# Zero-padded attention scores, a mask added on VectorE, a late softmax factor, and pooled products issued between the attention steps

## The chip, the cores and the metric

The kernel runs on one core of a Trainium2 chip, as one launch. The metric is the time of that launch on the device in microseconds, the median of several runs. TensorE is called PE, VectorE DVE, ScalarE ACT, GpSimd POOL and the DMA-issuing SyncE SP, as the profile has them.

## What is computed

Two small transformer stacks one after the other on 512 tokens of width 1024, all in float32. The first has a gated mixer with a linear recurrence and a feed-forward block. The second has two layers, each a SwiGLU block, a mixer and another SwiGLU block, where a vector `c` gives shifts, scales and gates through nine modulation products per layer (`w_ada`, 2 x 36 loads of 1 MB). The mixer of its first layer is the one that matters here: differential attention beside a multi-scale pooling branch.

```python
def probs(q, k):                       # 4 heads, two score maps each, 64 wide
    sc = einsum('bhqd,bhkd->bhqk', q, k) * scale
    sc = where(mask, sc, -inf)         # causal
    return softmax(sc)
w = probs(qa, k1) - lam * probs(qb, k2)
o = rmsnorm(einsum('bhqk,bhkd->bhqd', w, v), subln_g) * (1 - lam_init)
# pooling: four groups g, windows 2, 4, 8, 16 over the tokens
d = (cumsum - lagged cumsum) / count - u[g]
p = concat(d @ pool_w[g]) * pool_scale
x = x + gate * (concat([o, p]) @ w_out)
```

## The kernel before, in words

`Net` holds the residual transposed, as 8 blocks of 128 channels by 512 tokens. A weight block comes by one DMA on SP into a staging tile (`wload`, line 99), is split there into a rounded part `whi` (ACT, line 113) and a rest `wlo` (DVE, line 114), and a product is three matmuls per 128-row slice, `whi` with both parts of the input and `wlo` with the first (`mm3`, lines 124 to 126; in token order lines 146 to 148). Each call of `wblock` also runs one waiting step of the modulation products (`ada_step`, line 181): a 1 MB load into the one tile `ada` (line 638) and two DVE passes over 1024 columns (line 640). The order on each engine is set by the tile framework's scheduler, from the order in which the program is written; each engine then runs its own list in order, and waits on the others by semaphores.

`attn` (line 665) makes q, k and v, normalises q and k, and transposes them 128 tokens at a time (`finish`, line 719) into `qT` and `kT`. In these, the 128 partitions of one head hold the first score map's 64 channels and then the second's. `pool_unit` (line 740) makes one group's input `u` (24 matmuls of 512 columns) and its window sums on POOL (line 752), and `pool_out` (line 763) multiplies by `pool_w` (line 767).

The attention itself is 16 steps, (query block i, head h), i from 3 down to 0. Step s issues four stages, each of another step: `stA` of step s, `stB` of s-1, `stC` of s-2, `stD` of s-3. One score tile of `stA`, with n = 128 (i + 1) keys, is

```python
nc.tensor.matmul(ps[:, 0:i * 128], lhsT=ql, rhs=kr[pr, h % 2, 0:i * 128], ...)       # 64 rows, L790
nc.tensor.matmul(ps[:, i * 128:n], lhsT=ql, rhs=kr[pr, h % 2, i * 128:n], ...)       # 64 rows, L791
nc.tensor.matmul(ps[:, i * 128:n], lhsT=self.ident, rhs=cm, start=False, stop=True)  # mask, L792
```

followed by the row maximum (DVE, line 793) and the exponential with its sum (ACT, line 795). There are two tiles per step, 32 in all, in 5 PSUM buffers (`acc`). `stB` normalises and subtracts the two maps (DVE, lines 803 to 806) and transposes the result (PE, line 810; ACT, line 812). `stC` multiplies by v (PE, line 819) and normalises (ACT 822, DVE 85, POOL 86, DVE 824). `stD` transposes into `oT` (PE 830, ACT 833, DVE 834). After the steps 2, 6, 10 and 14 the loop issues one `pool_out`, and after the first three of these a whole `pool_unit`; the first `pool_unit` stands ahead of the loop. The output product (`down`, line 248) follows.

Of the kernel before, what the change touches and what calls it, by code (L numbers as in the profile page):

```python
# [9 lines left out]
F32 = mybir.dt.float32  # L10
F32R = mybir.dt.float32r
U8 = mybir.dt.uint8
AF = mybir.ActivationFunctionType
# [13 lines left out]
class Net:  # L27
    def __init__(self, ctx, tc, a, out):
        self.ctx, self.tc, self.nc, self.a, self.out = ctx, tc, tc.nc, a, out
        pool = lambda name, bufs, **kw: ctx.enter_context(tc.tile_pool(name=name, bufs=bufs, **kw))  # L30
        self.const = pool("const", 1)
        self.act = pool("act", 20)
        self.xv = pool("xv", 4)
        self.stg = pool("stg", 2)
        self.whl = pool("whl", 4)
        self.work = pool("work", 2)
        self.acc_p = pool("acc", 5, space=PSUM)
        self.ms_p = pool("ms", 3, space=PSUM)
        self.ada_todo = []
        self.setup()  # L40
# [87 lines left out]
    def gemm(self, wus, xs, t0=0, tn=512):  # L128
        pss = [self.acc() for _ in wus]
        n = len(xs)  # L130
        for k in range(n):
            for ps, wu in zip(pss, wus):
                self.mm3(ps, wu, k, xs[k], t0, tn, k == 0, k == n - 1)
        return pss
# [46 lines left out]
    def ada_step(self):  # L181
        if self.ada_todo:
            self.ada_todo.pop(0)()
# [64 lines left out]
    def down(self, src, kn, xs, gcol, nxt=None):  # L248
# [14 lines left out]
        for m in range(8 if nxt is None else 6):  # L263
            if m % 2 == 0:
                ws = blk(m // 2)
            ps = self.gemm([ws[m % 2]], xs)[0]
# [398 lines left out]
    def attn(self, hs, nxt, gcol):  # L665
        nc, a, tc = self.nc, self.a, self.tc
        with ExitStack() as es:
# [5 lines left out]
            cm = ap.tile([128, 128], F32, name="cmask")  # L673
            nc.gpsimd.dma_start(out=cm, in_=a["cmask"])
# [17 lines left out]
            tms = [pair("qT"), pair("kT"), pair("avt")]  # L692

            def qk_evac(w):
# [14 lines left out]
                def finish():  # L709
                    tt = tms[w]  # L710
                    for tb in range(4):
                        q = qs[tb]
                        nc.vector.tensor_tensor(
                            out=q.rearrange("p (h d) -> p h d", d=64), in0=q.rearrange("p (h d) -> p h d", d=64),
                            in1=rr[:, 8 * tb:8 * tb + 8].rearrange("p (h o) -> p h o", o=1).to_broadcast([128, 8, 64]),
                            op=ALU.mult)
                        pt = self.ms()
                        for h in range(4):
                            nc.tensor.transpose(pt[:, h * 128:(h + 1) * 128], q[:, h * 128:(h + 1) * 128], self.ident)
                        for i in range(2):  # L720
                            nc.scalar.copy(tt[i][:, :, tb * 128:(tb + 1) * 128],
                                           pt[:, 256 * i:256 * i + 256].rearrange("p (h t) -> p h t", h=2))
# [7 lines left out]
            qT, kT, vt = tms  # L730
# [8 lines left out]

            def pool_unit(g):  # L740
                if g % 2 == 0:
                    wu[:] = self.wblock(a["w_u"][g // 2], [(8, 128)] * 2)
                pu = self.gemm([wu[g % 2]], hs)[0]
                bufs = [ap.tile([128, 528], F32, tag=f"pl{i}", name="pl", bufs=1) for i in range(3)]
                for b in bufs:
                    nc.gpsimd.memset(b[:, 0:16], 0.0)
                u = bufs[0]
                nc.scalar.copy(u[:, 16:528], pu)
                cur = u
                for j in range(g + 1):  # L750
                    dst = bufs[1 + j % 2]
                    nc.gpsimd.tensor_tensor(out=dst[:, 16:528], in0=cur[:, 16:528], in1=cur[:, 16 - (1 << j):528 - (1 << j)],
                                            op=ALU.add)
                    cur = dst
                dv = self.wk("e2")
                nc.vector.scalar_tensor_tensor(out=dv[:, 16:512], in0=cur[:, 32:528], scalar=1.0 / (2 << g),
                                               in1=u[:, 32:528], op0=ALU.mult, op1=ALU.subtract)
                t = self.wk("plt", (128, 16), 2)
                nc.vector.tensor_tensor(out=t, in0=cur[:, 16:32], in1=rc[:, g, :], op=ALU.mult)
                nc.vector.tensor_tensor(out=dv[:, 0:16], in0=t, in1=u[:, 16:32], op=ALU.subtract)  # L760
                return dv

            def pool_out(g, dv):
# [3 lines left out]
                nc.tensor.matmul(py, lhsT=pw, rhs=dv, start=True, stop=True)  # L767
# [7 lines left out]
            dv = pool_unit(0)  # L775
# [5 lines left out]
            def stA(i, h):  # L781
                n = (i + 1) * 128
                st = self.wk("ast", (128, 8), 6)
                ws = []
                for e in range(2):
                    ps = self.acc()
                    pr = slice(64 * e, 64 * e + 64)
                    ql, kr = qT[h // 2][pr, h % 2, i * 128:n], kT[h // 2]
                    if i:
                        nc.tensor.matmul(ps[:, 0:i * 128], lhsT=ql, rhs=kr[pr, h % 2, 0:i * 128], start=True, stop=True)  # L790
                    nc.tensor.matmul(ps[:, i * 128:n], lhsT=ql, rhs=kr[pr, h % 2, i * 128:n], start=True, stop=False)  # L791
# [8 lines left out]
            def stB(i, h):  # L800
# [14 lines left out]
            def stC(i, h):  # L815
# [6 lines left out]
                nc.scalar.activation(out=o[:, 0, :], in_=po[:, 0:128], func=AF.Square, accum_out=st[:, 6:7])  # L822
                self.rstd(st[:, 7:8], st[:, 6:7], 1, 1.0 / 128)
                nc.vector.tensor_scalar(out=o[:, 1, :], in0=po[:, 0:128], scalar1=st[:, 7:8], scalar2=None, op0=ALU.mult)
# [12 lines left out]
            for s in range(len(steps) + 3):  # L837
# [175 lines left out]
```

## Time and profile before

| | us |
|---|---|
| runs | 2776.01, 2777.94, 2781.38 |
| median | 2777.94 |
| span of the profiled execution | 2777.7 |
| PE busy (matmul) | 2744.4 |
| DVE busy | 1379.4 |
| ACT busy | 852.5 |
| POOL busy | 211.3 |

The page gives no time of its own for the profiled execution beside its span. Attention lies between 1362.0 us (first score matmul) and 1457.1 us (last of `oT` written). Times on the axis are us from the span's start. A PE matmul's duration includes its pipeline, so the price of one in a row of many is the distance of the starts. A float32 matmul shows as two records (`x2`). "PEclk" is the clock granted to PE as a share of full speed: 1.00 is 2.4 GHz and 0.50 is 1.2 GHz.

### The profile page before, as it was taken

Reading aid. Unit: us, or ns where it says so; the run is one execution under the profiler, and the core shown is the slowest. Engines: PE = TensorE matmul, PEld = TensorE weight load, DVE = VectorE, ACT = ScalarE, POOL = GpSimd, SP = SyncE. Lnnn points to the kernel's source line nnn. Section 1 sums busy time; section 2 is a strip of 40 time slices with the busy share of each in tenths; the row PEclk is TensorE's granted clock in tenths of the full one; section 3 lists DMA queues with packets and bytes.
Section 4 is the critical chain, followed back from the end, with each engine's and each line's share of the span. In section 5 each row is a group of like instructions: output and inputs, shape, how many; then the busy total and the mean of one; then the engine's idle time right before and its main releaser. Section 6 shows DMA issues by size and latency. Waiting matters only on the chain.

```text
span 2777.7 us, 32460 instructions
## 1 busy us (share of the span) xinstructions
PE 2744.4 (99%) x13428; PEld 2308.1 (83%) x13428; DVE 1379.4 (50%) x2117; ACT 852.5 (31%) x1278; POOL 211.3 (8%) x187
## 2 busy tenths in 40 slices
PE   7999999999999999999999999999999999999999
PEld 6888888888888888888779888888888898888888
DVE  6655633476556755558555333344333354533333
ACT  5222232343224322224344222233222332332221
POOL 3000010200002000002131000010000111200000
PEclk9999999999999999999889999999999999999999
DMA  4211132365555455555202222222223222232222
GB/s 154 80 61 61 35 114 95 108 229 190 195 191 187 171 188 182 205 180 184 102 32 76 102 96 99 89 98 95 91 99 103 88 91 92 91 107 91 99 99 76
DMA packets 50307, 327.99 MB, mean 118 GB/s; under 512 B 5728, under 2 KB 6240, under 8 KB 15856
## 3 DMA queue, kind: packets, MB, share of 16 engines
q1 hardware_dynamic: 49248, 322.98, 33.3%
q0 software_dynamic: 912, 2.95, 0.3%
q8 instruction: 105, 1.72, 0.3%
q14 instruction: 42, 0.34, 0.0%
HBM read 323.81 MB, written 2.10 MB: 117 GB/s over the span
## 4 chain that ended last, share of the span: by engine, by line
PE 95%; DVE 1%; DMA 1%; POOL 1%; ACT 0%; issue 0%; DVEq 0%; POOLq 0%; ACTq 0%
PE acc L124 28%; PE acc L125 28%; PE acc L126 28%; PE ms L452 2%; PE acc L146 1%; PE acc L148 1%; PE acc L147 1%; PE ms L490 1%; PE ms L210 1%; PE acc L790 1%; PE ms L97 0%; PE acc L792 0%; PE ms L819 0%; PE ms L430 0%; PE acc L791 0%
## 5 line engine op out<-in xcount | busy, mean ns | idle before, releaser
L113 ACT CAST whi<-w 128x1024 fp32r<-128x1024 f32 (+1 forms) x472 | 486.0, 1030 | 1573.7 <-PE acc L125 1440.7
L125 PE MATMUL acc<-h,whi 128*128 128x512 f32 (+1 forms) x2432 | 908.5, 375 | 1.4 <-DVE h L244 0.8
L124 PE MATMUL acc<-h,whi 128*128 128x512 f32 (+1 forms) x2432 | 904.7, 375 | 2.9 <-ACT h L240 2.0
L126 PE MATMUL acc<-h,wlo 128*128 128x512 f32 (+1 forms) x2432 | 906.3, 374 | 0.0
L114 DVE TENSOR_TENSOR wlo<-w,whi 128x1024 fp32r<-128x1024 f32 (+1 forms) x472 | 581.3, 1233 | 465.0 <-ACT whi L113 448.3
L125 PEld LDWEIGHTS acc<-h,whi 128*128 128x128 f32 x2432 | 458.9, 189 | 81.7 <-DVE h L241 1.5
L124 PEld LDWEIGHTS acc<-h,whi 128*128 128x128 f32 x2432 | 456.4, 189 | 84.1 <-ACT h L240 3.2
L126 PEld LDWEIGHTS acc<-h,wlo 128*128 128x128 f32 x2432 | 458.7, 189 | 80.2 <-issue 1.2
L124 PE MATMUL acc<-y,whi 128*128 128x512 f32 (+1 forms) x1112 | 414.7, 373 | 0.2 <-ACT y L178 0.2
L126 PE MATMUL acc<-y,wlo 128*128 128x512 f32 (+1 forms) x1112 | 414.8, 373 | 0.0
L125 PE MATMUL acc<-y,whi 128*128 128x512 f32 (+1 forms) x1112 | 414.3, 373 | 0.4 <-DVE y L179 0.4
L125 PEld LDWEIGHTS acc<-y,whi 128*128 128x128 f32 x1112 | 209.4, 188 | 37.8 <-DVE y L179 1.2
L124 PEld LDWEIGHTS acc<-y,whi 128*128 128x128 f32 x1112 | 209.4, 188 | 37.4 <-ACT y L178 0.6
L126 PEld LDWEIGHTS acc<-y,wlo 128*128 128x128 f32 x1112 | 209.4, 188 | 36.6
L640 DVE SCALAR_TENSOR_TENSOR ada<-ada,cb 128x1024 f32<-128x1024 f32 x144 | 178.6, 1247 | 110.4 <-DMA ada<-in_w_ada 109.2
L259 DVE SCALAR_TENSOR_TENSOR xt<-acc,dmod,xt 128x512 f32<-128x512 f32 (+1 forms) x124 | 86.6, 698 | 274.5 <-PE acc L126 274.5
L620 DVE TENSOR_TENSOR e<-acc,e 128x512 f32<-128x512 f32 (+1 forms) x96 | 62.0, 645 | 236.9 <-PE acc L126 236.6
L178 ACT CAST y<-e 128x512 fp32r<-128x512 f32 (+1 forms) x140 | 81.4, 583 | 62.1 <-DVE e L605 42.4
L179 DVE TENSOR_TENSOR y<-e,y 128x512 fp32r<-128x512 f32 (+1 forms) x140 | 89.2, 639 | 9.0 <-ACT y L178 8.9
L197 POOL COPY SS<-sq 128x512 f32<-128x512 f32 x9 | 7.8, 868 | 996.9 <-issue 649.7
L200 POOL TENSOR_TENSOR SS<-SS,sq 128x512 f32<-128x512 f32 x45 | 71.0, 1582 | 128.3 <-ACT sq L194 128.1
L452 PEld LDWEIGHTS ms<-kq 128*128 128x128 f32 x448 | 56.5, 191 | 8.6 <-DVE kq L471 4.1
(232 smaller groups left out, 2109.4 us busy)
## 6 DMA issues: line engine op xcount, KB each, us to landing
w<-in_w_gu SPq DMA_DIRECT2D x88, 1024.0 KB, 4.9
ada<-in_w_ada SPq DMA_DIRECT2D x72, 1024.0 KB, 6.3
w<-in_w_ff SPq DMA_DIRECT2D x32, 1024.0 KB, 4.8
w<-in_w_dn SPq DMA_DIRECT2D x32, 896.0 KB, 4.5
w<-in_w_dn SPq DMA_DIRECT2D x16, 1024.0 KB, 5.0
w<-in_w_fq SPq DMA_DIRECT2D x8, 1024.0 KB, 4.8
w<-in_w_gg SPq DMA_DIRECT2D x8, 1024.0 KB, 5.3
w<-in_w_cx SPq DMA_DIRECT2D x8, 1024.0 KB, 4.9
```

Of the source, the lines that this page charges most:

```text
L113: nc.scalar.copy(hi[:, :n], w[:, o:o + n])
L114: nc.vector.tensor_tensor(out=lo[:, :n], in0=w[:, o:o + n], in1=hi[:, :n].bitcast(F32), op=ALU.subtract)
L124: nc.tensor.matmul(o, lhsT=hi[:, k, :], rhs=x[:, 0, t0:t0 + tn], start=first, stop=False)
L125: nc.tensor.matmul(o, lhsT=hi[:, k, :], rhs=x[:, 1, t0:t0 + tn], start=False, stop=False)
L126: nc.tensor.matmul(o, lhsT=lo[:, k, :], rhs=x[:, 0, t0:t0 + tn], start=False, stop=last)
L178: nc.scalar.copy(h, src)
L179: nc.vector.tensor_tensor(out=dst[:, 1, t0:t0 + tn], in0=src, in1=h.bitcast(F32), op=ALU.subtract)
L200: nc.gpsimd.tensor_tensor(out=dst, in0=dst, in1=sq, op=ALU.add)
L259: nc.vector.scalar_tensor_tensor(out=x, in0=ps[:, :tn], scalar=gcol[:, m:m + 1], in1=x, op0=ALU.mult, op1=ALU.add)
L452: nc.tensor.matmul(ps[:, c * 64:(c + 1) * 64].rearrange("p (n b) -> p n b", b=b), lhsT=K[:, s], rhs=half(Q[:, s], 1), start=True, stop=True)
L620: nc.vector.tensor_tensor(out=y, in0=pss[1][:, :tn], in1=t, op=ALU.mult)
L640: nc.vector.scalar_tensor_tensor(out=w[:, i, :], in0=w[:, i, :], scalar=1.0, in1=cb, op0=ALU.mult, op1=ALU.mult, accum_out=self.mod[l][:, ...
```

## The change

q of the two maps goes to two tiles of full height: `qz0` has the first map's 64 rows and zeros below, `qz1` zeros and then the second map's rows. A score tile is then one matmul of 128 rows and n columns against the whole `kT`. `qz0` takes the `ada` tile, so the modulation steps are held while attention runs (`ada_hold`) and six of them move into the output product and the block behind it. The mask is 512 wide and is added by the DVE instruction that also finds the maximum; it writes the tile (negated) to SBUF, where ACT takes the exponential. The factor 1 / (first sum) is left out of `stB` and applied in `stC` to the product. A `pool_unit` becomes a generator: six of its matmuls are issued at the end of each of the steps 0 to 11 (and the first unit's four pieces ahead of the loop), and `pool_out` comes after the steps 1, 5, 9 and 13. `down` takes the four `pT` slices first.

```diff
+    def gemm_steps(self, wu, xs, out, per=2):
+        ps = self.acc()
...
+            if k % per == per - 1:
+                if k == n - 1:
+                    out(ps)
+                yield
...
-        if self.ada_todo:
+        if self.ada_todo and not self.ada_hold:
...
-            cm = ap.tile([128, 128], F32, name="cmask")
-            nc.gpsimd.dma_start(out=cm, in_=a["cmask"])
+            cm = ap.tile([128, 512], F32, name="cmask")
+            nc.gpsimd.memset(cm[:, 0:384], 0.0)
+            nc.gpsimd.dma_start(out=cm[:, 384:512], in_=a["cmask"])
...
+            qz0 = self.ada_p.tile([128, 2, 1024], F32, tag="w", name="qz0", bufs=1).rearrange(
+                "p a (b t) -> p (a b) t", t=512)
+            qz1, kT, vt = pair("qz1"), pair("kT"), pair("avt")
+            nc.gpsimd.memset(qz0[64:128], 0.0)
+            for q in qz1:
+                nc.gpsimd.memset(q[0:64], 0.0)
...
+                        if w == 0:
+                            nc.scalar.copy(qz0[0:64, :, ts], pv[0:64])
+                            for i in range(2):
+                                nc.scalar.copy(qz1[i][64:128, :, ts], pv[64:128, 2 * i:2 * i + 2, :])
...
+                yield from self.gemm_steps(wu[g % 2], hs, window)
...
-                    pr = slice(64 * e, 64 * e + 64)
...
-                    nc.tensor.matmul(ps[:, i * 128:n], lhsT=self.ident, rhs=cm, start=False, stop=True)
-                    nc.vector.tensor_reduce(out=st[:, e:e + 1], in_=ps[:, :n], axis=AX.X, op=ALU.max, negate=True)
+                    nc.tensor.matmul(ps[:, 0:n], lhsT=qs[e], rhs=kT[h // 2][:, h % 2, 0:n], start=True, stop=True)
                     w = ap.tile([128, 512], F32, tag="aw", name="aw", bufs=4)
-                    nc.scalar.activation(out=w[:, :n], in_=ps[:, :n], func=AF.Exp, bias=st[:, e:e + 1],
+                    nc.vector.tensor_tensor_reduce(out=w[:, :n], in0=ps[:, :n], in1=cm[:, 512 - n:512], scale=-1.0,
+                                                   scalar=-NEG, op0=ALU.add, op1=ALU.min, accum_out=st[:, e:e + 1])
+                    nc.scalar.activation(out=w[:, :n], in_=w[:, :n], func=AF.Exp, bias=st[:, e:e + 1], scale=-1.0,
                                          accum_out=st[:, 2 + e:3 + e])
...
-                nc.vector.tensor_scalar(out=ws[1][:, :n], in0=ws[1][:, :n], scalar1=st[:, 5:6], scalar2=nlam,
+                nc.vector.tensor_scalar(out=st[:, 5:6], in0=st[:, 5:6], scalar1=st[:, 2:3], scalar2=nlam,
                                         op0=ALU.mult, op1=ALU.mult)
-                nc.vector.scalar_tensor_tensor(out=ws[0][:, :n], in0=ws[0][:, :n], scalar=st[:, 4:5],
-                                               in1=ws[1][:, :n], op0=ALU.mult, op1=ALU.add)
+                nc.vector.scalar_tensor_tensor(out=ws[0][:, :n], in0=ws[1][:, :n], scalar=st[:, 5:6],
+                                               in1=ws[0][:, :n], op0=ALU.mult, op1=ALU.add)
...
-                if s in (2, 6, 10, 14):
-                    pool_out(s // 4, dv)
-                    if s < 14:
-                        dv = pool_unit(s // 4 + 1)
-            return self.down(a["w_oab"], 8, oT + pT, gcol, nxt)
+                    if d == 0 and s < 12:
+                        next(pu, None)
+                if s in (1, 5, 9, 13):
+                    pool_out(s // 4)
+            self.ada_hold = False
+            return self.down(a["w_oab"], 8, oT + pT, gcol, nxt, [4, 5, 6, 7, 0, 1, 2, 3])
```

How the scheduler orders the two kernels is seen at three places. First PE where attention begins, right behind the transposes of k (`ms<-ident,qn`); the score tiles are `acc<-kT,...`, the pooled group's matmuls `acc<-h,...`, `ms<-ident,aw` transposes a finished map. Before:

```order
L719 MATMUL ms<-ident,qn 128x128 x16
L790 MATMUL acc<-kT,qT 128x384
L791 MATMUL acc<-kT,qT 128x128
L792 MATMUL acc<-cmask,ident 128x128
L790 MATMUL acc<-kT,qT 128x384
L791 MATMUL acc<-kT,qT 128x128
L792 MATMUL acc<-cmask,ident 128x128
```

and in the changed kernel:

```order
L736 MATMUL ms<-ident,qn 128x128 x16
L821 MATMUL acc<-kT,qz_9375 128x512
L821 MATMUL acc<-kT,qz_9376 128x512
L125 MATMUL acc<-h,whi 128x512
L126 MATMUL acc<-h,whi 128x512
L127 MATMUL acc<-h,wlo 128x512
L125 MATMUL acc<-h,whi 128x512
L126 MATMUL acc<-h,whi 128x512
L127 MATMUL acc<-h,wlo 128x512
L821 MATMUL acc<-kT,qz_9375 128x512
```

Three instructions of a tile became one, and six matmuls of the second pooled group stand behind every pair of tiles.

Second SP, the list of loads around attention (`w_u` pooled input, `w_oab` output product, `w_gu` the block behind it). Before:

```order
L638 DMA ada<-in_w_ada 128x2048
L101 DMA w<-in_w_u 128x2048
L638 DMA ada<-in_w_ada 128x2048
L101 DMA w<-in_w_u 128x2048
L101 DMA w<-in_w_oab 128x2048 x4
L101 DMA w<-in_w_gu 128x2048 x8
```

and in the changed kernel:

```order
L102 DMA w<-in_w_qkv 128x2048 x5
L102 DMA w<-in_w_u 128x2048 x2
L102 DMA w<-in_w_oab 128x2048 x4
L649 DMA ada<-in_w_ada 128x2048 x3
L102 DMA w<-in_w_gu 128x2048
L649 DMA ada<-in_w_ada 128x2048
```

The loads of `ada` moved behind those of `w_oab`; the first of them waits for PE, since the tile holds `qz0` until the last score matmul.

Third DVE at the end of attention, in the changed kernel (`aw<-aw,ast` is `stB`, `rs_t` and `ht` are `stC`, `oT` is `stD`, `ada` a moved modulation pass):

```order
L836 SCALAR_TENSOR_TENSOR aw<-aw,ast 128x128
L833 RECIPROCAL ast<-ast 128x2
L651 SCALAR_TENSOR_TENSOR ada,mod_4055<-ada,cb 128x1024
L86 TENSOR_SCALAR rs_t<-ast 128x1
L834 TENSOR_SCALAR ast<-ast,lam 128x1
L866 SCALAR_TENSOR_TENSOR oT<-ms,sublng,oT 128x128
L855 TENSOR_SCALAR ht<-ms,ast 128x128
L836 SCALAR_TENSOR_TENSOR aw<-aw,ast 128x128
L651 SCALAR_TENSOR_TENSOR ada,mod_4055<-ada,cb 128x1024
L86 TENSOR_SCALAR rs_t<-ast 128x1
L866 SCALAR_TENSOR_TENSOR oT<-ms,sublng,oT 128x128
L855 TENSOR_SCALAR ht<-ms,ast 128x128
```

Two modulation passes, the first of which waits for the load of `ada`, stand ahead of the last steps' `stB` to `stD`; before there was none in attention.

## Rows read from the trace of the kernel before

**Rows 1.** The page, part 1: busy us (share of the span) and instructions.

```profile
PE 2744.4 (99%) x13428; PEld 2308.1 (83%) x13428; DVE 1379.4 (50%) x2117; ACT 852.5 (31%) x1278; POOL 211.3 (8%) x187
```

**Rows 2.** Windows: us, then busy PE, PEld, DVE, ACT, POOL, clock, DMA share, GB/s.

```profile
1362.00:1363.70 1.70, 1.68 (x7) 1.16 (x8) 1.70 (x4) 0.80 (x3) 0.00 (x0) 1.00 0.00 0
1363.70:1380.70 17.00, 17.00 (x40) 10.57 (x40) 8.58 (x17) 5.16 (x13) 0.22 (x2) 0.50 0.18 62
1380.70:1438.80 58.10, 56.87 (x308) 43.52 (x306) 32.99 (x91) 27.95 (x87) 18.95 (x27) 1.00 0.12 39
1438.80:1455.90 17.10, 14.96 (x46) 10.62 (x47) 9.64 (x38) 7.89 (x37) 3.29 (x6) 0.50 0.00 0
1455.90:1457.10 1.20, 1.20 (x7) 0.81 (x7) 0.41 (x2) 0.73 (x2) 0.00 (x0) 1.00 0.00 0
1362.00:1457.10 95.10, 91.71 (x404) 66.67 (x405) 53.32 (x149) 42.52 (x141) 22.47 (x35) 0.82 0.11 35
```

**Rows 3.** Timeline of PE at full clock: start us, us, instruction.

```profile
1386.60 0.39 PE L125 MATMUL acc<-h,whi 128*128 128x512 f32 x1
1386.82 0.39 PE L126 MATMUL acc<-h,wlo 128*128 128x512 f32 x1
1387.14 0.91 PE L790 MATMUL acc<-kT,qT 64*128 64x384 f32 x2
1387.89 0.38 PE L791 MATMUL acc<-kT,qT 64*128 64x128 f32 x2
1388.20 0.49 PE L792 MATMUL acc<-cmask,ident 128*128 128x128 f32 x2
1388.62 0.91 PE L790 MATMUL acc<-kT,qT 64*128 64x384 f32 x2
...
1390.00 0.60 PE L810 MATMUL ms<-ident,aw 128*128 128x128 f32 x4
1390.44 1.06 PE L819 MATMUL ms<-avt,awT 128*128 128x128 f32 x8
1391.33 0.27 PE L830 MATMUL ms<-ident,ht 128*128 128x128 f32 x1
1391.54 0.70 PE L790 MATMUL acc<-kT,qT 64*128 64x256 f32 x2
...
1392.80 0.70 PE L790 MATMUL acc<-kT,qT 64*128 64x256 f32 x2
```

**Rows 4.** The chain that ended last, in order of time: start us, us, what.

```profile
1382.72 0.86 PE ms L767 x2
```

**Rows 5.** Groups by line and shape, 1362.0 to 1457.1: busy us, mean ns, idle before.

```profile
L752 POOL TENSOR_TENSOR pl<-pl 128x512 f32<-128x512 f32 x9 | 11.6, 1283 | 14.2 <-ACT pl L748 13.8
L86 POOL TENSOR_TENSOR ast<-rs_t,mhalf 128x1 f32<-128x1 f32 x16 | 9.0, 564 | 51.5 <-DVE rs_t L85 40.2 <-DVE ast L803 11.3
L114 DVE TENSOR_TENSOR wlo<-w,whi 128x1024 fp32r<-128x1024 f32 x5 | 6.9, 1388 | 6.5 <-ACT whi L113 6.5
L795 ACT ACTIVATION_READ_ACCUMULATOR aw<-acc,ast 128x1 f32 x32 | 6.4, 201 | 0.0
L824 DVE TENSOR_SCALAR ht<-ms,ast 128x128 f32<-128x128 f32 x16 | 5.6, 350 | 7.1 <-POOL ast L86 7.1
L795 ACT ACTIVATE aw<-acc,ast 128x512 f32<-128x512 f32 x8 | 5.5, 688 | 8.7 <-DVE ast L793 8.7
L793 DVE TENSOR_REDUCE ast<-acc 128x1 f32<-128x512 f32 x8 | 5.5, 687 | 8.1 <-PE acc L792 8.1
L771 DVE SCALAR_TENSOR_TENSOR pT<-ms,cols,pT 128x512 fp32r<-128x512 f32 x4 | 3.0, 751 | 1.2 <-ACT pT L770 1.1
L803 DVE RECIPROCAL ast<-ast 128x2 f32<-128x2 f32 x16 | 2.5, 156 | 1.1 <-ACT aw L795 1.1
L793 DVE TENSOR_REDUCE ast<-acc 128x1 f32<-128x128 f32 x8 | 2.2, 279 | 1.0 <-PE acc L792 1.0
```

**Rows 6.** Instructions on the tile `ada`, 1280 to 1400: load to landing.

```profile
DMA to landing us min/median/max: 4.7/4.8/5.1
```

More of the change, by code (lines that the diff above doesn't have):

```diff
@@ L126, in mm3, with gemm @@
         nc.tensor.matmul(o, lhsT=lo[:, k, :], rhs=x[:, 0, t0:t0 + tn], start=False, stop=last)
-    def gemm(self, wus, xs, t0=0, tn=512):
+    def gemm(self, wus, xs, t0=0, tn=512, order=None):
         pss = [self.acc() for _ in wus]
+        ks = order or range(len(xs))
+        for k in ks:
+            for ps, wu in zip(pss, wus):
+                self.mm3(ps, wu, k, xs[k], t0, tn, k == ks[0], k == ks[-1])
+        return pss
+    def gemm_steps(self, wu, xs, out, per=2):
+        ps = self.acc()
         n = len(xs)
         for k in range(n):
-            for ps, wu in zip(pss, wus):
-                self.mm3(ps, wu, k, xs[k], t0, tn, k == 0, k == n - 1)
-        return pss
+            self.mm3(ps, wu, k, xs[k], 0, 512, k == 0, k == n - 1)
+            if k % per == per - 1:
+                if k == n - 1:
+                    out(ps)
+                yield
     def gemm_tok_steps(self, srcs, xs, evac, us=None):
@@ L246, in norm_half, with down @@
         return r
-    def down(self, src, kn, xs, gcol, nxt=None):
+    def down(self, src, kn, xs, gcol, nxt=None, order=None):
         nc = self.nc
@@ L265, in down @@
                 ws = blk(m // 2)
-            ps = self.gemm([ws[m % 2]], xs)[0]
+            ps = self.gemm([ws[m % 2]], xs, order=order)[0]
             upd(m, ps, 0, 512)
@@ L738, in attn @@
             wu = []
+            dvs = {}
             def pool_unit(g):
@@ L742, in pool_unit @@
                     wu[:] = self.wblock(a["w_u"][g // 2], [(8, 128)] * 2)
[L743 to L761, printed above, removed]
@@ L763, in pool_out, with window @@
-            def pool_out(g, dv):
+                def window(pu):
+                    bufs = [ap.tile([128, 528], F32, tag=f"pl{i}", name="pl", bufs=1) for i in range(3)]
+                    for b in bufs:
+                        nc.gpsimd.memset(b[:, 0:16], 0.0)
+                    u = bufs[0]
+                    nc.scalar.copy(u[:, 16:528], pu)
+                    cur = u
+                    for j in range(g + 1):
+                        dst = bufs[1 + j % 2]
+                        nc.gpsimd.tensor_tensor(out=dst[:, 16:528], in0=cur[:, 16:528],
+                                                in1=cur[:, 16 - (1 << j):528 - (1 << j)], op=ALU.add)
+                        cur = dst
+                    dv = self.wk("e2")
+                    nc.vector.scalar_tensor_tensor(out=dv[:, 16:512], in0=cur[:, 32:528], scalar=1.0 / (2 << g),
+                                                   in1=u[:, 32:528], op0=ALU.mult, op1=ALU.subtract)
+                    t = self.wk("plt", (128, 16), 2)
+                    nc.vector.tensor_tensor(out=t, in0=cur[:, 16:32], in1=rc[:, g, :], op=ALU.mult)
+                    nc.vector.tensor_tensor(out=dv[:, 0:16], in0=t, in1=u[:, 16:32], op=ALU.subtract)
+                    dvs[g] = dv
@@ L764, in pool_out, with pools @@
+                yield from self.gemm_steps(wu[g % 2], hs, window)
+            def pools():
+                for g in range(4):
+                    yield from pool_unit(g)
+            def pool_out(g):
                 py = self.ms()
@@ L766, in pool_out @@
                 nc.gpsimd.dma_start(out=pw, in_=a["pool_w"][:, g, :])
-                nc.tensor.matmul(py, lhsT=pw, rhs=dv, start=True, stop=True)
+                nc.tensor.matmul(py, lhsT=pw, rhs=dvs.pop(g), start=True, stop=True)
                 d = self.slot("pT")
@@ L773, in pool_out @@
                 pT.append(d)
-            dv = pool_unit(0)
+            pu = pools()
+            for _ in range(4):
+                next(pu)
             fk()
```

24 lines of the change are left out of this document (12 added, 12 removed).

## The prediction

> **What bounds the kernel now.** I read the page first: PE is busy for 2744 of 2778 us [rows 1], so time is won only where PE does less, waits, or runs slowly. The table of windows finds such a place: in the 95.1 us of attention PE's clock was granted at 1.00 except in two stretches of 17.0 and 17.1 us at 0.50, that is at 1.2 instead of 2.4 GHz [rows 2]. The first began 1.7 us after the first score matmul, while PE was busy without a break (17.00 of 17.00 us); the second began in the last query block's steps, where PE also waited (14.96 of 17.10). Between them, with the same kinds of matmul but pooled products of 512 columns among them, the clock stayed at 1.00 for 58.1 us. Counted at full clock, PE's work in attention is 1.7 + 17.0/2 + 56.9 + 15.0/2 + 1.2 = 75.7 us. The 19.4 us up to 95.1 are the slow clock (8.5 + 7.5) and waits (3.4).
>
> The timeline then gives prices as distances of starts. A 512-key score tile takes 1.48 us from its first start to that of the next tile: 0.75 for 384 columns, 0.31 for 128, 0.42 for the mask [rows 3]. A 384-key tile takes 1.26 [rows 3], so 128 columns cost 0.22 and every tile carries 0.62 that does not depend on its width. A full float32 matmul of 512 columns takes 0.86 [rows 4], which is 0.215 for 128 columns.
>
> **The change part by part.**
>
> *Score tiles.* The mask matmul and the split at the diagonal go; what stays is one stream of n columns. A tile falls from 1.48 to 0.86, from 1.26 to 0.65, and the two smaller ones by the same 0.62 (what is left is 0.44 and 0.22). 32 tiles x 0.62 = 19.8 us of PE work. That leaves 55.9 of the 75.7.
>
> The Trainium skill, "TensorE: Matmul & The Clock Gate", Part 3 (packing small matmuls), says that matmuls on different row groups of the array run at the same time, which speaks against padding 64 rows to 128. By it, 8.6 us would be lost, and the sum below would give 2763. Rows 3 don't agree: 384 columns of 64 rows took 0.75, not less than the 0.645 of 384 full columns by rows 4, and no tile's parts start together; so I take the rows.
>
> *Clock.* Every pair of tiles is now followed by six pooled matmuls (0.22 apart [rows 3], 1.35 us), as in the 58.1 us that kept 1.00. So I expect neither long slow stretch. How soon it recovers if it falls once behind the k transposes, or in the last steps, no row of before shows: the bounds are nothing and the 16.0 us lost now [rows 2]. I take 3 us, nearer the lower end, since the middle stretch is what the changed order resembles most.
>
> *DVE.* With less on PE, DVE sets the pace of many steps. The fused mask-and-maximum pass is in no row. Its lower bound is the reduction, 0.69 at 512 columns and 0.28 at 128, 0.136 for each 128 [rows 5]; its upper bound is that plus an elementwise pass of 0.75, 1.44 [rows 5]. I take 0.75, the price of one pass from PSUM with a second operand [rows 5], to which it is closest. A 512-key step is then two such passes, one subtraction of 0.75 (the scaling over n columns becomes one column), three small ones of 0.156 and two of 0.35 [rows 5]: 3.4 us. Every four steps also bring a weight split of 1.39, a pooled result of 0.75, a pass for the window sums taken as 0.75, and two small ones [rows 5]: 0.8 a step. And where the reciprocal stands right behind the second tile's pass, DVE waits out ACT's exponential and its sum, 0.69 + 0.20 [rows 5]. With that wait a step is 5.1, and 0.54 less for each 128 keys fewer (four passes of 0.136): 4 x (5.1 + 4.6 + 4.0 + 3.5) = 69 us. Without it DVE needs 4.2, 3.8, 3.4, 3.0.
>
> PE needs in a 512-key step 1.72 for tiles, 1.35 for pooled matmuls, 0.44 + 0.89 + 0.21 for transposes and the product with v [rows 3], and 0.22 as the share of `pool_w` [rows 4]: 4.8, then 4.1, 3.3 and, without pooled matmuls, 1.2. The larger of the two in each step gives 4 x (4.8 + 4.1 + 3.4 + 3.0) = 61 us. Between 61 and 69 I take 65.
>
> *The end.* Behind the last scores the last step still passes through all stages, some 4.5 us at 128 columns (estimate from rows 5: exponential 0.6, subtraction 0.35, small ones 0.5, three ACT passes near 0.3, POOL 0.56, two DVE passes of 0.35, the rest PE). And there is a new wait: the moved load of `ada` may start only when the last score matmul has read `qz0`; it takes 4.8 us [rows 6]. DVE reaches its first modulation pass about 2.5 us after that matmul, and everything of the last steps stands behind it. So some 2.3 us of wait and two passes of 1.3 (as the 1024-column split, 1.39 [rows 5]), 5 us; bounds 1 and 7. PE can meanwhile run the output product's `pT` slices, and by the order has issued 38 of its matmuls before the last transpose, against 11 before the change: 27 x 0.225 = 6.1 us that need not follow.
>
> *Beside other work.* The zeroing on POOL is ahead of the q product, where POOL is nearly idle; the two maps' copies add about 2 us on ACT under the v product; the held modulation passes (twelve, 15 us of DVE) move to a stretch where PE has a backlog. POOL's window adds are as before, 1.28 each, and can hold up the 0.56 of `stC` [rows 5] as they do now. I cost these at nothing; if a cover fails, it is by 1 to 2 us each.
>
> *Sum.* 65 + 4.5 + 5 - 6.1 + 3 (clock) = 71.4 us where 95.1 were: 23.7 us less. Against the profiled span of 2777.7 that is 2754.0; the median of the runs, 2777.9, is 0.2 higher, which is within the rounding: **2754 us**.
>
> **The rivals.**
>
> - *PE alone decides* (chance 0.10): the order hides the waits of DVE and no long wait for `ada` comes. 61 + 4.5 + 1 - 6.1 = 60.4, 34.7 less: 2743. For it: in the middle stretch PE was idle for only 1.2 of 58.1 us [rows 2]. Against: PE has lost a third of its work per step and DVE little.
> - *The clock falls as before* (0.08): the 16 transposes and the thin last steps bring back both slow stretches, so 16.0 instead of 3, of which DVE's pace hides a few: about 2764.
> - *The fused pass is two passes* (0.10): 0.69, 0.55, 0.41 and 0.28 more for 8 tiles each, 15.4 us on an engine that sets the pace: 2769.
> - *The halves ran together* (0.02): two 64-row tiles overlapped and the padded ones stream twice as much, 10,240 columns x 0.86/512 / 2 = 8.6 us: 2763. Against it stand the starts in rows 3. It is the skill's rule cited above.
> - *The moved modulation passes are not hidden* (0.06): they delay the normalisation behind the output product or its weight loads; the 15 us come back, and with them most of the gain: 2769 to 2778.
> - *Slower: the clock stays low all through* (0.06). Full-height float32 tiles with zeros, transposes and gaps of DVE's making keep PE at 0.50, as the 17 us of uninterrupted work did [rows 2]. PE's 55.9 us then take 112, and with 4.5 us of drain attention lasts 116: 21 us longer, 2799. It decides from about half: with some 10 us of waits, 55.9 x (1 + f) + 10 passes 95.1 at f = 0.52.
>
> **How the numbers follow.** The forecast keeps 0.58; its own range is 2746 to 2762 (61 to 69 us of steps and 1 to 7 of the wait). The range of 2743 to 2769 takes in the first four rivals and leaves out the last, part of the modulation rival, and edges of the fused pass: under 0.2. A measurement of this kernel can tell about 0.2%, 5.6 us, from no change. Faster by more than that are the forecast, the first four rivals and a third of the modulation one, less a rest for two mishaps at once: 0.89. Same 0.05, slower 0.06.
>
> **What would show it.** Right: the two stretches at 0.50 gone or a few us long; score tiles at 0.86 from start to start; attention some 70 us long; the waits on PE behind DVE, one near the end behind the load of `ada`. Wrong: a long stretch at 0.50, a fused pass well over 0.8 us at 512 columns, or new PE idling in the output product or ahead of the q product.

## The result, and the profile after

| | before | changed |
|---|---|---|
| runs, us | 2772.21, 2776.01, 2776.92, 2777.94, 2781.38 | 2760.53, 2760.75, 2762.82, 2763.88, 2766.63 |
| median, us | 2776.92 | 2762.82 |
| ratio, 95% interval | | 0.9948, 0.9934 to 0.9963 |
| span of the traced execution | 2777.7 | 2758.8 |
| first score matmul to last product matmul | 139.10 | 115.10 |

The changed kernel is faster by 14.1 us in the medians, 0.5%. The forecast was 2754, the range 2743 to 2769. The time printed for the traced execution is 2760.75, 1.95 more than its span.

I compare one stretch in all traces: from the first score matmul to the start of the last matmul of the output product, so that work which moves between the two counts once. Behind it all traces agree: 1276.6 us to the end. First part 1 of the page of the changed kernel, to be read with [rows 1]: PE is still the engine that is busy nearly all the time.

```profile
PE 2715.3 (98%) x13316; PEld 2287.1 (83%) x13316; DVE 1378.9 (50%) x2149; ACT 856.0 (31%) x1282; POOL 210.7 (8%) x191
```

The stretch in the table of windows, columns as in [rows 2]. Before:

```profile
1362.02:1501.12 139.10, 135.29 (x646) 104.75 (x647) 70.35 (x172) 55.95 (x160) 32.23 (x44) 0.88 0.14 47
```

and in the changed kernel, in its parts and as a whole:

```profile
1367.12:1425.80 58.68, 50.07 (x247) 36.94 (x247) 40.59 (x135) 33.67 (x102) 16.32 (x28) 1.00 0.16 51
1425.80:1432.60 6.80, 5.73 (x20) 4.78 (x21) 4.33 (x21) 2.90 (x14) 2.31 (x3) 0.50 0.50 206
1432.60:1444.40 11.80, 11.34 (x53) 7.68 (x52) 8.88 (x31) 6.08 (x25) 2.74 (x5) 1.00 0.24 74
1367.12:1482.22 115.10, 104.52 (x534) 82.41 (x534) 81.19 (x225) 55.69 (x157) 30.50 (x44) 0.97 0.31 111
```

The stretch is 24.0 us shorter, and it divides into three. Half of PE's busy time at 0.50 is what I count as the cost of the clock: 8.5 + 7.5 = 16.0 before [rows 2], 5.73/2 = 2.9 now. PE's work at full clock is then 135.3 - 16.0 = 119.3 before and 104.5 - 2.9 = 101.6 now. What is left of the length is idling: 3.8 before, 10.6 now. So **work -17.7, slow clock -13.1, idling +6.8**.

Where PE idles in attention, and what DVE waits for there (table of waits: engine, tile, line, behind whom, us in total, times, longest):

```profile
PE ms L840 <- DVE aw L836: 3.0, 1, 3.0
PE ms L862 <- DVE ht L855: 2.4, 2, 2.1
PE ms L849 <- DVE oT L866: 2.1, 1, 2.1
PE ms L798 <- ACT awT L842: 1.6, 1, 1.6
```

```profile
DVE ast L833 <- ACT aw L825: 6.7, 7, 1.0
DVE ht L855 <- POOL ast L87: 6.6, 15, 1.6
DVE e L781 <- POOL pl L777: 5.3, 3, 2.1
```

DVE waited for POOL before the change too:

```profile
DVE ast L793 <- PE acc L792: 12.7, 8, 3.0
DVE ht L824 <- POOL ast L86: 7.1, 14, 2.4
DVE e L756 <- POOL pl L752: 4.3, 3, 2.2
```

Its waits on POOL were 7.1 + 4.3 = 11.4 us and are 6.6 + 5.3 = 11.9 now. What is new is that PE idles behind them. Before, DVE also waited 12.7 us for PE's score tiles (5.9 in E6's trace), a wait that is gone, and PE had work of its own while DVE stood still: during DVE's longest wait for `e`, from 1413.10 to 1415.35, PE was busy for 2.25 of 2.25 us with score tiles. The timeline of the changed kernel shows how the wait reaches PE now:

```profile
1384.62 2.70 POOL L777 TENSOR_TENSOR pl<-pl 128x512 f32<-128x512 f32 x2 [3.28 <-ACT pl L773]
...
1387.35 0.68 DVE L781 SCALAR_TENSOR_TENSOR e<-pl 128x496 f32<-128x496 f32 x1 [2.05 <-POOL pl L777]
...
1388.65 0.34 DVE L866 SCALAR_TENSOR_TENSOR oT<-ms,sublng,oT 128x128 fp32r<-128x128 f32 x1
...
1389.04 1.16 PE L849 MATMUL ms<-avt,awT 128*128 128x128 f32 x8 [2.05 <-DVE oT L866]
```

POOL is in the window adds of a pooled group. DVE has the use of their result, `e`, next in its list and stands still for 2.05 us; the fused passes and `oT` are queued behind it, and PE waits as long. At 1408.75 the next group's `e` waits 2.14 us, and PE 2.05 behind `ht`. At 1425.16 it is POOL's power `ast` that comes late, behind two adds; `ht` waits 1.56 us for it, and PE 2.98 behind `aw`.

Prices that the prediction had to guess, from the groups by line and shape: the fused pass over 512 and 128 x 384 elements, and its accumulator read.

```profile
L823 DVE CUSTOM_DVE_ANT_0 aw<-acc,cmask 128x512 f32<-128x512 f32 x8 | 5.2, 684 | 0.0
L823 DVE CUSTOM_DVE_ANT_0 aw<-acc,cmask 128x384 f32<-128x384 f32 x8 | 4.3, 551 | 0.0
L823 DVE DVE_READ_ACCUMULATOR2_ANT ast<- 128x1 f32 x32 | 2.7, 83 | 0.0
```

The whole span is shorter by 18.9 us only, because attention starts 5.10 us later, at 1367.12 instead of 1362.02. 0.4 of them are there before 1125 us. 4.0 arise at 1134 us, in a feed-forward block whose instructions are the same and in the same order in both kernels. Before, PE waited there for `y` 0.16 us; in the trace after:

```profile
1131.89 1.23 DVE L651 SCALAR_TENSOR_TENSOR ada<-ada,cb 128x1024 f32<-128x1024 f32 x1 [6.01 <-DMA ada<-in_w_ada]
...
1134.43 0.50 PE L125 MATMUL acc<-y,whi 128*128 128x512 f32 x1 [2.48 <-ACT y L189]
```

```profile
1135.66:1139.07 3.41, 3.41 (x9) 2.65 (x9) 2.51 (x4) 0.94 (x1) 0.00 (x0) 0.50 0.91 305
```

A load of `ada` landed late, DVE and through `y` PE waited for it, and 3.4 us at half clock followed. The last 84 us ahead of attention are 0.4 us longer in the changed kernel, in both of its traces (84.8 against 84.4 in the two traces of the kernel before): there the first score matmul waits 0.7 us for the copies of k instead of 0.2.

### The profile page after: what moved, and what is told of

Read it like the earlier page. It is cut to its first block, busy times and chain, and to the rows that moved or that the text cites. A ratio compares the mean times of both kernels' runs of the same rounds, so it can differ in the third digit from the quotient of the medians.

```text
span 2758.8 us, 32263 instructions
## 1 busy us (share of the span) xinstructions
PE 2715.3 (98%) x13316; PEld 2287.1 (83%) x13316; DVE 1378.9 (50%) x2149; ACT 856.0 (31%) x1282; POOL 210.7 (8%) x191
## 4 chain that ended last, share of the span: by engine, by line
PE 91%; DVE 3%; DMA 1%; POOL 1%; issue 1%; ACT 1%; POOLq 0%; ACTq 0%; DVEq 0%
PE acc L125 28%; PE acc L126 28%; PE acc L127 28%; PE ms L463 2%; PE acc L159 1%; DMA ada<-in_w_ada 1%; PE acc L157 1%; PE acc L158 1%; PE ms L501 1%; PE ms L221 1%; PE ms L98 0%; POOL pl L777 0%; PE ms L441 0%; DVE wlo L115 0%; ACT aw L825 0%
## 5 line engine op out<-in xcount | busy, mean ns | idle before, releaser
L126 PE MATMUL acc<-h,whi 128*128 128x512 f32 (+1 forms) x2432 | 907.9, 374 | 1.4 <-DVE h L255 0.8
L126 PEld LDWEIGHTS acc<-h,whi 128*128 128x128 f32 x2432 | 458.8, 189 | 82.6 <-issue 1.9
L126 PE MATMUL acc<-y,whi 128*128 128x512 f32 (+1 forms) x1112 | 414.8, 373 | 0.9 <-DVE y L190 0.9
L126 PEld LDWEIGHTS acc<-y,whi 128*128 128x128 f32 x1112 | 209.8, 189 | 38.4 <-DVE y L190 1.6
```

Source lines behind the costliest of these rows:

```text
L126: nc.tensor.matmul(o, lhsT=hi[:, k, :], rhs=x[:, 1, t0:t0 + tn], start=False, stop=False)
```

## Experiments

Each group ran on one chip beside the kernel before. Its medians were 2775.55 (E1 to E4), 2782.16 (E5 to E8) and 2773.12 us (E9 to E11); ratios are to that kernel in the same group. "Idle" is the stretch's length less PE's busy time; "at 0.50" is the time at half clock inside the stretch of the traced execution.

| kernel | median, us | ratio, 95% interval | stretch | idle | at 0.50 |
|---|---|---|---|---|---|
| before, first trace | | | 139.10 | 3.8 | 34.1 |
| before, second (E6) | 2775.48 (one run) | | 130.77 | 3.5 | 17.1 |
| changed, first trace | 2762.82 | 0.9948, 0.9934 to 0.9963 | 115.10 | 10.6 | 6.8 |
| changed, second (E5) | 2756.65 | 0.9916, 0.9902 to 0.9930 | 115.25 | 10.6 | 6.8 |
| E1 `e` later | 2755.81 | 0.9926, 0.9911 to 0.9941 | 113.75 | 9.3 | 3.4 |
| E2 bulk | 2762.40 | 0.9948, 0.9935 to 0.9961 | 118.79 | 12.6 | 6.8 |
| E3 64 rows | 2763.90 | 0.9957, 0.9941 to 0.9973 | 117.31 | 13.3 | 13.7 |
| E4 64 rows, bulk | 2768.12 | 0.9967, 0.9951 to 0.9984 | 124.92 | 16.1 | 27.3 |
| E7 adds spread | 2752.15 | 0.9893, 0.9878 to 0.9907 | 108.95 | 6.0 | 0 |
| E11, the same again | 2752.59 | 0.9908, 0.9882 to 0.9933 | 108.49 | 5.8 | 0 |
| E8 old product order | 2767.40 | 0.9945, 0.9930 to 0.9959 | 122.90 | 15.0 | 17.1 |
| E9 before, `pT` first | 2770.61 | 0.9984, 0.9965 to 1.0004 | 126.28 | 2.4 | 6.8 |
| E10 spread, 64 rows | 2753.75 | 0.9920, 0.9894 to 0.9946 | 112.04 | 6.6 | 10.2 |

**E1, the use of the window sums queued later** (`fins[g]` holds DVE's three instructions for group g; group 0 stays where it was).

```diff
+                    last[i, h] = nc.vector.tensor_tensor_reduce(...)
...
-                if s in (1, 5, 9, 13):
+                if s in (4, 9, 13):
+                    with tc.issue_after(last[steps[s]].ins):
+                        fins.pop(s // 4)()
+                if s in (1, 5, 10, 14):
                     pool_out(s // 4)
```

> The changed kernel with one edit: the three VectorE instructions that end a pooled group's window sums (`e`, `plt`, `e`) are queued behind the second fused pass of step 4, 9 and 13 (groups 1 to 3) instead of standing where the scheduler put them, one step or so earlier, and pool_out follows after the steps 5, 10 and 14. Theory: in the changed kernel VectorE stands idle in front of `e` for 2.05 us (step 4) and 1.16 us (the last group) because POOL's window adds are late, everything of the attention behind it in VectorE's list waits, and PE idles 2.05 us at 1389.0 and 2.98 at 1426.6; the last of these idles is followed by the 6.8 us at half clock. With `e` queued later these waits go: 4 to 5 us of PE idling and up to 3.4 us of slow clock, so 2755 to 2759 against 2762.8 for the changed kernel. Rival: VectorE sets the pace of these steps anyway (11.5 to 15 us busy of 16 to 22), so the idling only moves to other steps: 2761 to 2764, and the slow clock comes somewhere else in the last steps.

The time is in the theory's range, its reason is not. PE idles 9.3 us instead of 10.6: the waits on `e` shrank (5.3 to 1.2 us), but those on POOL's power grew by 3.0:

```profile
DVE ht L860 <- POOL ast L87: 9.6, 14, 2.7
...
DVE e L786 <- POOL pl L777: 1.2, 1, 1.2
```

As the rival had it, the idling moved. The ratio lies between the two of the changed kernel, 0.9948 and 0.9916, and cannot be told from them. What it showed is the next thing in the way: the run of adds itself, in POOL's list.

**E2, pooled units in one piece behind the steps 2, 6 and 10.**

```diff
-                    if d == 0 and s < 12:
-                        next(pu, None)
-                if s in (1, 5, 9, 13):
+                if s in (2, 6, 10, 14):
                     pool_out(s // 4)
+                    for _ in range(4):
+                        next(pu, None)
```

> The changed kernel with the pooled products not issued between the steps: a whole pooled unit of 24 matmuls follows the steps 2, 6 and 10 and pool_out the steps 2, 6, 10 and 14, as before the change; zero padding, VectorE mask and late factor stay. Theory: what keeps the clock at full in the first query block is the pooled matmuls between the score tiles. Without them the clock falls to 0.50 near the first score matmul for some 17 us as it did before, and VectorE's pace leaves PE idle in the steps that have no pooled work; 8.5 us of clock and a few us of idling: 2770 to 2780. Rival: the full-height, single-stream tiles keep the clock; then only the order changes and the time is 2761 to 2768, with no long stretch at 0.50 in the first block.

The rival held: no fall of the clock in the first block. Twelve records of score tiles stand in a row there, then PE waits; the window is at 1.00 throughout:

```profile
1369.10:1376.00 6.90, 6.08 (x18) 2.84 (x18) 6.43 (x18) 3.26 (x9) 0.22 (x2) 1.00 0.45 152
```

By the two traces the interleaving saved 2.0 us of idling, and not the clock; the times do not show it, the ratio is that of the changed kernel's first comparison.

**E3, q in 64 rows.** The zero padding, `qz0` and its zeroing are gone, so the held loads of `ada` also run ahead of attention again.

```diff
-                    nc.tensor.matmul(ps[:, 0:n], lhsT=qs[e], rhs=kT[h // 2][:, h % 2, 0:n], start=True, stop=True)
+                    nc.tensor.matmul(ps[:, 0:n], lhsT=qT[h // 2][64 * e:64 * e + 64, h % 2, i * 128:n],
+                                     rhs=kT[h // 2][64 * e:64 * e + 64, h % 2, 0:n], start=True, stop=True)
```

> The changed kernel without the zero padding: q goes into two tiles as before (64 rows for each map), a score tile is one matmul of 64 rows and n columns; the tile `qz0` and its zeroing are gone, the rest (mask on VectorE, late factor, pooled matmuls between the steps, modulation steps held) stays. Theory: PE's price of a tile goes by its columns, not its rows, and the clock is kept by the pooled matmuls, so nothing changes: 2760 to 2766, tiles 0.86 us from start to start at 512 columns. Rival 1: full height is what keeps the clock; then a stretch of some 17 us at 0.50 comes back in the first block: 2768 to 2773. Rival 2: the two halves of the array work at the same time when both tiles have 64 rows; PE then wins up to 8.6 us, of which VectorE's pace lets part through: 2754 to 2760, and the second tile's start lies less than 0.86 behind the first's.

The time is that of the theory, and the first block kept 1.00 without full height (13.7 us at 0.50 come later in the stretch). But rival 2's mechanism is there. PE's timeline of a pair of 512-column tiles in the changed kernel, and then in E3:

```profile
1370.33 1.88 PE L821 MATMUL acc<-kT,qz 128*128 128x512 f32 x4
1371.64 0.80 PE L125 MATMUL acc<-h,whi 128*128 128x512 f32 x1
1372.28 0.40 PE L126 MATMUL acc<-h,whi 128*128 128x512 f32 x1
```

```profile
1369.45 1.13 PE L810 MATMUL acc<-kT,qT 64*128 64x512 f32 x4
1370.51 0.50 PE L125 MATMUL acc<-h,whi 128*128 128x512 f32 x1
1370.85 0.40 PE L126 MATMUL acc<-h,whi 128*128 128x512 f32 x1
```

From the pair's start to the second product matmul (L126) are 1.95 us with padding and 1.40 with 64 rows: the two halves started 0.007 us apart, ran together and won 0.55. Over the stretch PE's work at full clock is 3.0 us less than in the changed kernel (98.6 against 101.6), its idling 2.7 us more and the cost of the clock 2.6 more; what PE won, it waited.

**E4, 64 rows and pooled units in one piece** (both edits above).

> Neither zero padding nor pooled products between the steps; the mask on VectorE and the late factor are all that is left of the change (with the output product's order and the held modulation steps). Theory (clock by the pooled matmuls): the same as with padding and bulk units, within 3 us. Rival (clock by the full height): clearly slower than that kernel by the 8 us of a slow stretch that padding avoids. In both, against the kernel before: about 24 us of PE's matmul work less at full clock, of which slow clock and VectorE's pace take some back: 2765 to 2775.

Slower than E2 by 5.7 us, between the 3 us of the theory and the 8 of the rival, with four stretches at 0.50. Its idling is the largest, 16.1 us. With neither of the two parts the clock fell in the first block for 3.4 us, 6.8 us behind the first score matmul. Either part alone held the first block at 1.00, neither held the last steps; and the kernel before, which has neither, also kept 1.00 in the first block in one execution (E6). Which part keeps the clock is not settled.

**E5, the changed kernel again**, and **E6, the kernel before again.**

> The changed kernel as it is, for another execution's trace and more times on one chip with the others of this group. Theory: the stretch from the first score matmul to the output product's last (115.1 us in the first trace of the changed kernel, 139.1 before the change) is set by the program up to a few us, the slow clock in it and the wait of 2.48 us at 1134 us (ahead of anything changed) differ from execution to execution; so 113 to 119 us for that stretch, 0 to 17 us of it at half clock, and a median of 2760 to 2765. Rival: the first trace is what every execution does: 115.1 +- 0.5, one stretch of 6.8 us at half clock behind an idle of 3 us, and again 2.5 us of wait at 1134.

> The kernel before the change as it is, for another execution's trace. The rows of the first one have 34.1 us at half clock in attention, 16.0 us of the time. Its later runs show a mean granted clock from 0.986 to 0.996 where the traced one had 0.991, so theory: this execution has less slow clock in attention, 10 to 27 us, its first score matmul to the output product's last matmul lasts 130 to 137 us instead of 139.1, and part of the gain that the two first traces show was the traced execution's. Rival: the two stretches of 17 us belong to the program: 34 us at half clock and 139 us again.

E5 repeats the stretch to 0.15 us, with the same idles and again 6.8 us at 0.50 behind the idle of 2.98:

```profile
1362.26:1477.51 115.25, 104.63 (x533) 82.38 (x534) 81.27 (x225) 55.70 (x157) 30.49 (x44) 0.97 0.32 111
```

The wait at 1134 us is gone, and one of 1.63 stands at 1247 instead, again in unchanged code. So in the stretch the rival is right, outside it the theory; the median, 2756.65, is below the 2760 to 2765 of the theory. E6 settles the larger question:

```profile
1366.19:1434.17 67.98, 67.13 (x351) 50.46 (x351) 42.20 (x105) 33.61 (x102) 19.18 (x29) 1.00 0.15 49
1434.17:1451.24 17.07, 14.92 (x47) 10.39 (x47) 10.29 (x42) 8.12 (x37) 2.75 (x5) 0.50 0.00 0
1366.19:1496.96 130.77, 127.32 (x645) 100.12 (x646) 70.31 (x172) 55.90 (x160) 32.20 (x44) 0.93 0.15 50
```

The first slow stretch of [rows 2] is not there, the second is, to the same 17.07 us. Half of the slow clock that the prediction counted on was in one execution and not in the other.

**E7, the window adds one at a time**, and **E11, the same again.**

```diff
+                for _ in range({4: 1, 5: 1, 8: 1, 9: 1, 10: 1, 12: 1, 13: 2, 14: 1}.get(s, 0)):
+                    with tc.issue_after(last["C" if len(adds) > 1 else "A"].ins):
+                        adds.pop(0)()
+                if s in (1, 6, 11, 14):
+                    pool_out(s // 5 if s < 14 else 3)
```

`adds` holds the adds of one group and last its use on DVE; "C" is the latest power on POOL, "A" the latest fused pass. So E1's part, the use queued later, is in this edit too.

> The changed kernel with POOL's window adds spread over the steps, one behind each step's `ast` power (two in step 13) instead of in one run, the VectorE end of the window behind the fused pass of step 5, 10 and 14, and pool_out after the steps 6, 11 and 14. Theory: after the late `e` was cured, what kept PE idle was `ht` behind POOL's power, which stood behind two to four window adds of 1.3 us (9.6 us of VectorE waiting, 2.34, 1.90 and 1.76 us of PE idling). With at most one add in front of a power these idles go: 4 to 6 us less than with `e` moved alone, 2749 to 2753. Rival: VectorE's and ACT's own work sets the pace: 2754 to 2757, the idling elsewhere.

> The kernel with the spread window adds as it ran before (2752.15 us there, its first score matmul to the output product's last matmul 108.95 us, no slow clock in it), for the comparison on one chip with the others of this group and for a second trace. Theory: 107 to 111 us for that stretch again and at most 4 us of slow clock in it; 0.988 to 0.991 of the kernel before. Rival: the first run was a lucky one: 113 us or more, 0.992 or above.

Both as the theory had them. (E11's interval, up to 0.9933, also takes in its rival's 0.992; the stretch decides.) The stretch, in two executions on two chips, has no slow clock:

```profile
1366.26:1475.21 108.95, 102.93 (x534) 80.00 (x535) 82.40 (x225) 55.48 (x157) 33.29 (x44) 1.00 0.35 118
```

```profile
1379.94:1488.43 108.49, 102.67 (x533) 79.92 (x534) 82.36 (x225) 55.51 (x157) 33.30 (x44) 1.00 0.35 118
```

and the waits of DVE on POOL are short ones (E7; the longest were 1.6 and 2.1 us in the changed kernel):

```profile
DVE ht L862 <- POOL ast L87: 5.5, 15, 0.7
...
DVE e L788 <- POOL pl L783: 1.5, 2, 0.9
```

This version beats both kernels: 4.5 us below the changed kernel in the same group, where each of its four times is below each of the six of E5, and 30.0 below the one before (20.5 in E11's group). Its ratio also lies clear of E1's, so the spread adds do more than the later use alone. The execution of E11 that was traced is its slowest, 2767.14, and by what lies ahead of the stretch, which begins at 1379.94.

**E8, the output product's old order** (`oT` first).

```diff
-            return self.down(a["w_oab"], 8, oT + pT, gcol, nxt, [4, 5, 6, 7, 0, 1, 2, 3])
+            return self.down(a["w_oab"], 8, oT + pT, gcol, nxt)
```

> The changed kernel with the output product's slices in the old order, `oT` ahead of `pT`. Theory (the term of 6.1 us in the sum): without `pT` first PE has little to do while the last steps pass through their stages, the 34 product matmuls that ran ahead of the last transpose of `ht` become some 9, and 25 x 0.225 = 5.6 us come back; thin steps with idling may also bring more slow clock: 2766 to 2772. Rival: the scheduler or the last steps on VectorE hide it: 2761 to 2764.

As the theory had it: 10.8 us slower than E5 in the medians, 7.65 in the stretch. (Between the two traces another 4.3 us lie ahead of attention, in unchanged code.) 10 product matmuls instead of 34 stand ahead of the last transpose of `ht`, and the stretch at 0.50 in the last steps is back to 17.07 us:

```profile
1424.87:1441.94 17.07, 11.32 (x33) 7.32 (x34) 11.84 (x48) 7.50 (x32) 4.85 (x7) 0.50 0.34 129
1366.55:1489.45 122.90, 107.91 (x533) 84.08 (x534) 81.72 (x224) 56.03 (x158) 30.49 (x44) 0.93 0.29 104
```

By the same account as above against E5, idling is 4.4 of the 7.65 and the clock 11.32/2 - 6.04/2 = 2.6 (6.04 is PE's busy time in E5's slow stretch).

**E9, that order in the kernel before.**

> The kernel before the change with one part of it: the output product takes its `pT` slices first. Theory: the slow clock of the last steps comes where PE has no product to fill them; undoing this order in the changed kernel brought a stretch of 17 us at half clock back and cost 10.8 us in the medians. So here the last steps get some 30 product matmuls ahead of the last transpose instead of 9, the second slow stretch goes or shrinks to some 7 us, and 6 to 12 us of the time go: 0.9955 to 0.998 of the kernel before. Rival: with the old tiles PE has enough work of its own there (14.96 of 17.10 us busy), so only the 4 to 5 us of product work that run ahead count and the slow stretch stays: 0.998 to 1.000.

23 product matmuls run ahead instead of 9 and the second slow stretch is 6.8 us instead of 17.1; the stretch is 4.5 us below E6's. In the medians 2.5 us are left, and the interval includes no change. The trace goes with the theory, the times with the rival: not settled.

**E10, adds spread and 64 rows.**

> The kernel with the spread window adds, and q in 64 rows again (no zero padding, no `qz0`). Pairs of 512-column tiles then start 0.007 us apart and take 1.05 us together instead of 1.72, 6.6 us of PE work less over the 16 pairs. Theory: VectorE sets the pace of the steps, so the won time becomes idling, and less filled steps risk slow clock: within 3 us of the spread kernel with padding (its sibling in this group), not faster by over 2. Rival: with the window adds out of the way PE's work counts again: 4 to 7 us faster than the sibling.

As the theory had it in the times: not faster than E11, 1.2 us above it. Its reason, won time that becomes idling, shows only in part. The stretch of the trace:

```profile
1374.97:1487.01 112.04, 105.40 (x533) 78.13 (x534) 69.66 (x204) 56.55 (x158) 31.59 (x44) 0.95 0.18 58
```

PE was busy for 10.08 of the 10.2 us at 0.50, so its work at full clock is 105.4 - 5.0 = 100.4 us, 2.3 less than in E11. Idling took back 0.8 of it; the clock cost 5.0 us, and in E11 nothing. The traced execution is the slowest of E10's six, 2765.4; whether the others have slow clock there is open.

No run undoes the mask on DVE or the late factor alone, so what these two gave apart from the rest of the change is not shown.

## Why the prediction was right, and where it was off

The way from 2754 to 2762.8 can be followed step by step. 2754.0 was a span, and I set it equal to a time; what lies around the span is 1.95. The stretch gained 24.0 where 23.7 were forecast: -0.3. It starts 5.10 later, all but 0.4 of it by unchanged code. That makes 2760.75, the time of the traced execution; the median of its five runs is 2.07 higher.

- *Score tiles* (19.8): right. A padded pair and one product matmul take 1.95 us, 2 x 0.86 + 0.225. PE's work fell by 17.7; the 2.1 in between I did not separate.
- *"Rows 3 don't agree"*: this reading of the traces failed. In E3 the two 64-row halves of a pair took 1.40 us with the product behind them, against 1.95 with padding. The Trainium skill, "TensorE: Matmul & The Clock Gate", Part 3, says that matmuls on different row groups run at the same time, and E3's trace agrees: 0.007 us from start to start. Rows 3 could not show it: the 0.75 there is the price of one half alone, and a full-height mask matmul stood between the two halves of every pair; without it they stand side by side. The rival that rested on the overlap gave 2763, the median almost to the microsecond, and still for another reason: without padding the time was not better (E3, and E10 against E11). In E3 the won time came back as idling and as slow clock, in E10's trace mostly as slow clock.
- *Clock* (3 of 16 left): in the changed kernel's traces right, 6.8 us at 0.50 in each, which cost 2.9 and 3.0. The step that failed is "the 16.0 us lost now". Another execution of the kernel before lost 14.92/2 = 7.5, so 8.5 of the 16.0 belonged to the execution and not to the kernel. The runs say so too: span times mean granted clock, an estimate of the time at full clock, has a median of 2757.1, 2756.1 and 2756.7 us for the kernel before in the three groups, and 2745.3 (first runs) and 2747.2 (E5) for the changed one. That is 9 to 12 us of change by the program. (The product also halves PE's idling inside a slow stretch. By it E8 with 2747.6 and E5 with 2747.2 are the same, though E8's stretch has 4.4 us more idling.) What the clock took from the kernel before had medians of 16.6, 25.0 and 16.6 us; from the changed one 16.6 and 9.6. (The clock is given to 0.001, 2.8 us.) So the gain was 14.1 in the first comparison and 25.5 in E5's group.
- *DVE sets the pace, 65 of 61 to 69*: the sum was right, its parts partly by luck. From the first score matmul to the last of `oT` are 77.2 us; the terms gave 65 + 4.5 + 5 + 3 = 77.5 (the sign "some 70 us" left the 6.1 of the product in). At the last score matmul the 77.2 divide into 61.9 and 15.4, not into 65 and 9.5; before the change the second part was 15.0. The fused pass is 0.68 + 0.08, as taken. But *POOL's window adds*, costed at nothing, or 1 to 2 us if a cover fails, cost PE most of the 6.8 us of added idling: E7 took 4.6 us of idling and the slow clock behind it away. The adds are as before, as I wrote, and so are DVE's waits on POOL (11.4 and 11.9 us). What I missed is that the cover was PE's own score tiles, as the longest of these waits shows, and that the same change makes them cheaper.
- *The wait for `ada`* (5): it did not come. DVE's first pass starts at 1436.91 without a wait, and PE was busy for 11.34 of the last 11.80 us, with the last steps and the output product. That this over-estimate of 5 about equals what the missed adds cost is luck.
- *`pT` first* (-6.1): right in kind, E8 gives 7.65 in the stretch. By the order 38 matmuls were to run ahead, 11 before; the traces have 34 and 9. That this order also shortens the slow clock of the last steps I had not seen.
- *Costed at nothing*: right for the moved modulation passes, and 0.4 us for the copies ahead of attention. Behind the stretch both traces take 1276.6 us, though DVE waits 6.3 us for `ada` during the product.
- *Rivals*: "the clock falls as before" gave 2764, "the fused pass is two passes" 2769. The traces exclude both causes in the executions seen. "Slower: the clock stays low all through" did not occur.

## What to carry over

A stretch at half clock in one trace is a property of that execution until a second trace repeats it: before counting on its end, multiply each run's span by its mean granted clock, and see what is left of the difference. A cover is worth no more than the work that makes it: when a change takes work from the busiest engine, count again every wait of the others that this work hid. Where small products are threaded between latency-bound steps, look not only at the engine that gets them but at everything that finishes them; a 1.2 us add in POOL's list, or its use in DVE's, stops all that stands behind it. Time won on an engine that does not set the pace can come back as idling or as slow clock: the 64-row pairs were cheaper by 0.55 us, and the medians show no gain.

## What the hardware showed beyond that

Code that no edit touched varied more than the change's details. The second feed-forward product of the block ahead of attention, behind the same instructions in all these kernels, began at 1241.0 us in E5 and at 1260.5 in E11, mostly by half clock: ahead of attention E11 has 41.0 us of it (13.7 in one piece near the start) and E5 6.8. Waits for `ada` of up to 2.5 us come and go as well.

POOL and DVE slow each other. In E1 a `wlo` pass that began beside an add took 2.03 us, and a power that began beside this pass 1.38; alone they take 1.23 and 0.55:

```profile
1383.71 1.04 POOL L777 TENSOR_TENSOR pl<-pl 128x512 f32<-128x512 f32 x1
1383.80 2.03 DVE L115 TENSOR_TENSOR wlo<-w,whi 128x1024 fp32r<-128x1024 f32 x1
...
1384.87 1.38 POOL L87 TENSOR_TENSOR ast<-rs_t,mhalf 128x1 f32<-128x1 f32 x1
```

The Trainium skill, "GPSIMD Engine Reference", Specifications, says that POOL shares its interfaces to SBUF with VectorE, with contention where a DVE instruction has two SBUF inputs; `wlo` has two, and the trace agrees. Spreading the adds does not end it: in E7 a power beside a `wlo` pass took 1.47 us.
